# Eight heads of a gated recurrence: wide products queued in equal shares behind the score products of each level

## The chip, the cores and the metric

The kernel runs on one core of one Trainium2 chip, as one launch. The metric is the time of one execution on the device in microseconds (us); a kernel's time is the median of several runs. A profile shows one execution. Its engines are PE (TensorE, the matrix products), DVE (VectorE), ACT (ScalarE), POOL (GpSimd) and SP (SyncE, which here issues the DMAs). PEclk is the clock granted to TensorE as a share of 2.4 GHz.

## The reference

One layer of an encoder on x of 1024 positions by 1024 features, in float32. A first big product makes the inputs of two branches. Branch A is a gated linear recurrence with 8 heads of key and value size 128, run forwards and backwards; branch B is a gated MLP that mixes positions in chunks of 128. Both are merged under sigmoid gates, then come an output product, a SwiGLU and a last gated term. In short:

```
h = rms_norm(x);  z = h @ w_in                       # q, f_fwd, f_bwd, i, g, u, v, gate_a, gate_b
A = bidirectional_recurrence(q, f_fwd, f_bwd, i, g)  # 8 heads, S_t = diag(f_t) S_{t-1} + k_t v_t^T, o_t = S_t^T q_t
B = gelu(u) * mix_positions(layer_norm(gelu(v)))
mix = (sigmoid(gate_a) * (A @ w_a) + sigmoid(gate_b) * (B @ w_b)) @ w_out
x = x + rms_norm(mix);  x = x + rms_norm(swiglu(rms_norm(x)));  x = x + (p @ w_ple) * sigmoid(x @ w_ple_gate)
```

## The kernel before

Every wide product is done in three passes: each operand is split into a high and a low part (`split_into`: ScalarE copies the high part, VectorE or GpSimd subtracts for the low one), and `mm3` runs high by high, high by low and low by high for each 128 of the contraction. One such matmul is 128 x 128 by 128 x 512. The stages are: norm and first products; most columns of the first product by a seven-product scheme (`Seven`, line 283 of before for its matmuls); the head loop; the merge; the SwiGLU; the end.

The head loop runs over 8 heads. For a head, `load_head` fetches F (the forget factors of both directions), X and Y (keys) and q; `load_values` fetches v and zg. `scores` then builds the 128 x 128 score blocks of all 8 chunks without a sequential recurrence: a first group of products of q with ks = X + Y, and then seven levels (blocks of 1, 2, 4, ... 64 positions). A level is 8 small products of X with QA in two banks of PSUM called `sc`, 4 products each (TensorE shows each of these as two records). After each bank VectorE multiplies QA by the next factors of F (L612) and X likewise (L615), and merges the level's scores into SC under a mask (`copy_predicated`, L625) or ScalarE does (L622); GpSimd makes the next Y (L639), ScalarE copies it into X (L636), and VectorE halves F (L645). So QA of a level must be updated before the next level's products of the same bank, while X runs ahead by itself.

`outputs` turns the scores of a head into its output: transposes of X and Y (L662), products with v (L667), a chain of states S on VectorE (L671, L673), output products (L691), a norm over ScalarE, VectorE and GpSimd (L694, L104, L106, L698), transposes (L701), and a store to `at_d`. In the queue it falls beside the scores of the next head.

Beside each head stands wide work that has nothing to do with that head: `values` in heads 0 and 1 (counted from zero), `branch` in heads 2 and 3, `transpose_b` and a part of `branch_b` in head 4, the rest of `branch_b` in head 5, `gate_a(0)` and `gate_a(1)` in heads 6 and 7. Its products go to three PSUM banks called `mm`. The A halves that the merge needs (A0, A1) reuse the memory of h's halves, which the two calls of `gate_a` read.

What sets the order is a scheduler that goes by the program's order, the dependencies and a model of times; nothing in the kernel before says where in a head the wide work goes. Each engine then runs its queue in that order, and an instruction that waits holds up what is behind it.

Of the kernel before, what the change touches and what calls it, by code (L numbers as in the profile page):

```python
# [35 lines left out]
def kernel(ctx: ExitStack, tc: tile.TileContext, a: dict, out: bass.AP):  # L36
# [109 lines left out]
    def fm_rhs(fm):  # L146
        return lambda p, k: fm[p][k // 4][:, k % 4, :]
# [406 lines left out]
    c_t, t1 = phase("s1t", 2)  # L554
    c_tw, tmw = phase("tmw", 4)

    class Head:
        pass

    def view(t, off, dims):  # L560
        tv = t[:]
        return bass.AP(tv.tensor, tv.offset + off, [list(tv.ap[0])] + dims)
# [17 lines left out]
    def scores(h, s):  # L580
        q, X, Y, F = s.q, s.X, s.Y, s.F
        QA = hg.tile([P, 2, T], F32, name="QA", bufs=2)
        ks = hg.tile([P, T], F32, name="ks")
        SC = hg.tile([P, NT, P], F32, name="SC", bufs=2)
        nc.vector.tensor_tensor(out=QA, in0=view(q, 0, [[0, 2], [1, T]]), in1=F, op=ALU.mult)
        nc.vector.tensor_tensor(out=ks, in0=X, in1=Y, op=ALU.add)

        for g in range(2):
            sp = ps_tile("sc")
            for i in range(4):  # L590
                cs = slice((4 * g + i) * P, (4 * g + i + 1) * P)
                nc.tensor.matmul(sp[:, i * P:(i + 1) * P], lhsT=ks[:, cs], rhs=q[:, cs], start=True, stop=True)
            nc.scalar.activation(SC[:, 4 * g:4 * g + 4], sp.rearrange("p (c t) -> p c t", c=4), AF.Copy)

        for li, m in enumerate(LEVELS):
            nb = T // m
            cb = P // (2 * m)

            def level(g):
                sp = ps_tile("sc")  # L600
                for i in range(4):
                    c = 4 * g + i
                    nc.tensor.matmul(  # L603
                        sp[:, i * P:(i + 1) * P], lhsT=X[:, c * P:(c + 1) * P],
                        rhs=view(QA, c * P, [[2 * m, cb], [T + m, 2], [1, m]]), start=True, stop=True)
                return sp

            def update(g, X2):

                o, of = g * NH, g * nb // 2  # L610
                qd = [[T + m, 2], [2 * m, nb // 4], [1, m]]
                nc.vector.tensor_tensor(out=view(QA, o, qd), in0=view(QA, o, qd),  # L612
                                        in1=view(F, of + 1, [[nb - 1, 2], [2, nb // 4], [0, m]]), op=ALU.mult)
                dims = [[4 * m, nb // 8], [3 * m, 2], [1, m]]
                nc.vector.tensor_tensor(out=view(X2, o, dims), in0=view(X, o, dims),  # L615
                                        in1=view(F, nb + of + 1, [[4, nb // 8], [1 - nb, 2], [0, m]]), op=ALU.mult)

            def merge(g, sp):
                if m >= 32:
                    for p0 in range(0, P, m):  # L620
                        c0 = p0 ^ m
                        nc.scalar.activation(SC[p0:p0 + m, 4 * g:4 * g + 4, c0:c0 + m],  # L622
                                             sp.rearrange("p (c t) -> p c t", c=4)[p0:p0 + m, :, c0:c0 + m], AF.Copy)
                    return
                nc.vector.copy_predicated(  # L625
                    SC[:, 4 * g:4 * g + 4], masks[:, li, None, :].broadcast_to([P, 4, P]),
                    sp.rearrange("p (c t) -> p c t", c=4))

            X2 = hg.tile([P, T], F32, name="X", bufs=3)
            sp0 = level(0)  # L630
            update(0, X2)
            merge(0, sp0)
            sp1 = level(1)

            mid = [[4 * m, nb // 4], [1, 2 * m]]
            nc.scalar.activation(view(X2, m, mid), view(Y, m, mid), AF.Copy)  # L636
            update(1, X2)
            mid = [[4 * m, nb // 4], [m, 2], [1, m]]
            nc.gpsimd.tensor_tensor(out=view(Y, m, mid), in0=view(X, m, mid),  # L639
                                    in1=view(F, 0, [[4, nb // 4], [nb + 3, 2], [0, m]]), op=ALU.mult)  # L640
            X = X2
            merge(1, sp1)
            F2 = hg.tile([P, 2, nb // 2], F32, name=f"F{2 * m}", bufs=2 if m == 64 else 1)
            Fv = F.rearrange("p d (b h) -> p d b h", h=2)
            nc.vector.tensor_tensor(out=F2, in0=Fv[:, :, :, 0], in1=Fv[:, :, :, 1], op=ALU.mult)  # L645
            F = F2
        s.QA, s.SC, s.X, s.Y, s.F = QA, SC, X, Y, F
# [76 lines left out]

    def tm_tile(gi, t, per_tile):
        ps = ps_tile("mm")
        mm3(ps, fm_lhs(hT[t // 4], t % 4), lambda p, k: tw[gi][k // 2][:, p, k % 2, :], KD)
        per_tile(t, ps)

    def values(ts):  # L730
# [16 lines left out]
    def transpose_b(bT):  # L747
        for t in range(NT):
            if t % 2 == 0:
                raw = rawp.tile([P, 2, SGW], F32, name="ub", tag="raw")  # L750
                nc.sync.dma_start(raw, ub_d[t // 2])
            tp = ps_tile("mm")
            for i in range(4):
                nc.tensor.transpose(tp[:, i * P:(i + 1) * P], raw[:, t % 2, i * P:(i + 1) * P], ident)
            ts = slice(t % 4 * P, (t % 4 + 1) * P)
            split_into(bT[t // 4][0][:, :, ts], bT[t // 4][1][:, :, ts], tp.rearrange("p (k t) -> p k t", k=4))

    def branch_b(bT, js):
        for j0 in js:
            raw = rawp.tile([P, KD, P], F32, name="raw", tag="raw")  # L760
            for i in range(2):
                nc.sync.dma_start(raw[:, 4 * i:4 * i + 4], a["w_b"][j0 + i])
            wb = whlp.tile([P, 2, KD, P], F32R, name="whl", tag="whl")
            split_into(wb[:, 0], wb[:, 1], raw)
            for i in range(2):
                m0 = rawp.tile([P, T], F32, name="gb", tag="raw")
                nc.sync.dma_start(m0, gb_d[j0 + i])
                for n in range(2):
                    ns = slice(n * NH, (n + 1) * NH)
                    ps = ps_tile("mm")  # L770
                    mm3(ps, lambda p, k: wb[:, p, 4 * i + k, :], lambda p, k: bT[n][p][:, k, :], 4)
                    nc.vector.tensor_tensor(out=m0[:, ns], in0=ps, in1=m0[:, ns], op=ALU.mult)
                nc.sync.dma_start(m0_d[j0 + i], m0)

    def gate_a(n):
        for j in range(NGA, KD):
            w = load_split(a["w_fm"][24 + j], [KD, P], None, whlp, rawp)
            ps = ps_tile("mm")
            mm3(ps, lambda p, k: w[:, p, k, :], fm_rhs(hT[n]), KD)
            sg = t2(t1, "sk")  # L780
            nc.scalar.activation(sg, ps, AF.Sigmoid)
            nc.sync.dma_start(sig_d[j, :, n * NH:(n + 1) * NH], sg)
# [19 lines left out]
    for h in range(H):  # L802
        nxt = Head()
        scores(h, cur)
        if h + 1 < H:
            load_head(nxt, h + 1)
        if h < 2:
            if h == 1:
                tw[2] = [load_tm(2, kk, tmw, "tmw") for kk in (0, 1)]
# [5 lines left out]
        elif h == 4:  # L815
            bT = [pair(tmw, f"bT{n}", "tmw") for n in range(2)]
            transpose_b(bT)
            branch_b(bT, (0,))
        elif h == 5:
            branch_b(bT, (2, 4, 6))  # L820
        elif h == 6:

            gate_a(0)
# [335 lines left out]
```

## Time and profile before

| what | before |
|---|---|
| median of 3 runs | 2000.14 us (1999.91 to 2002.68) |
| the profiled execution | 1999.0 us, span 1997.2 us |
| TensorE busy | 1913.6 us, 96% of the span |
| VectorE busy | 1200.5 us, 60% |
| ScalarE, GpSimd busy | 737.7 us (37%), 203.7 us (10%) |
| mean granted TensorE clock | 0.982 |
| from the first score product to the merge | from 581.9 to about 1052 us of the span |

TensorE is busy for 96% of the span, so what matters is where the other 4% and the stretches of lower clock lie: of the page's 40 slices (49.9 us each) TensorE is below nine tenths only in the first, in the 14th and in the 18th to 21st, which is the second half of the head loop. A row of the timeline gives the start and the length of merged instructions; neighbours overlap a little, so the distance from start to start is what one costs in a stream.

### The profile page before, as it was taken

How to read it: one execution, taken by the hardware profiler on the slowest of the kernel's cores; microseconds unless marked ns; L12 is line 12 of the kernel's file. 1: busy time of each engine (PE TensorE's matmuls, PEld its weight loads, DVE VectorE, ACT ScalarE, POOL GpSimd, SP SyncE). 2: the span in 40 equal slices, each digit the busy share in tenths (PEclk: the TensorE clock that was granted, in tenths of full speed). 3: DMA queues.
4: the chain of work that ended last, by engine and by line, in shares of the span. 5: the costliest groups of instructions: out<-in, count | busy, mean ns of one | idle time of the engine just before them, and what ended most of it. 6: DMA issues, size and time to landing. Idle time of an engine off the chain costs nothing.

```text
span 1997.2 us, 24233 instructions
## 1 busy us (share of the span) xinstructions
PE 1913.6 (96%) x9168; PEld 1603.6 (80%) x9168; DVE 1200.5 (60%) x1870; ACT 737.7 (37%) x1383; POOL 203.7 (10%) x153
## 2 busy tenths in 40 slices
PE   7999999999999899987679999999999999999999
PEld 6878888888888888876667887788888888888887
DVE  6667756664336676788654367865545536545743
ACT  6245544443323323433332246433333324213321
POOL 2510000000022111223112201000000000001000
PEclk9999999999999999998879999999999999999999
DMA  7234434443252456443124323232222205324232
GB/s 278 70 126 154 158 128 137 138 147 113 82 207 100 159 189 231 134 141 118 43 86 167 127 89 117 91 108 70 95 85 74 85 32 194 106 75 155 89 105 80
DMA packets 94933, 243.83 MB, mean 122 GB/s; under 512 B 10080, under 2 KB 19424, under 8 KB 93792
## 3 DMA queue, kind: packets, MB, share of 16 engines
q1 hardware_dynamic: 94816, 242.28, 36.1%
q8 instruction: 72, 1.18, 0.3%
q14 instruction: 45, 0.37, 0.1%
HBM read 168.32 MB, written 73.92 MB: 121 GB/s over the span
## 4 chain that ended last, share of the span: by engine, by line
PE 87%; DVE 7%; DMA 3%; ACT 1%; issue 1%; POOL 0%; SPq 0%; DVEq 0%; ACTq 0%; POOLq 0%
PE ps_mm L283 24%; PE ps_mm L138 22%; PE ps_sc L283 12%; PE ps_sc L138 9%; PE ps_st L138 5%; PE ps_sc L603 4%; PE ps_o L283 2%; PE ps_tr L283 2%; PE ps_st L283 2%; DVE QA L612 2%; PE ps_o L691 2%; DVE X L615 1%; DMA m_d<-gb 1%; DVE SC L625 1%; PE ps_st L667 1%
## 5 line engine op out<-in xcount | busy, mean ns | idle before, releaser
L283 PE MATMUL ps_mm<-T,w 128*128 128x512 f32 x1584 | 378.5, 389 | 0.0
L283 PEld LDWEIGHTS ps_mm<-T,w 128*128 128x128 f32 x1584 | 297.3, 188 | 61.9 <-ACT u L233 0.2
L120 DVE TENSOR_TENSOR w<-sums,w 128x1024 fp32r<-128x1024 f32 x88 | 107.7, 1224 | 102.1 <-ACT w L119 102.1
L603 PE MATMUL ps_sc<-QA,X 128*128 128x128 f32 x896 | 133.3, 302 | 33.3 <-DVE QA L612 27.1
L603 PEld LDWEIGHTS ps_sc<-QA,X 128*128 128x128 f32 x896 | 124.1, 208 | 40.9 <-DVE QA L612 16.6
L119 ACT ACTIVATE w<-sums 128x1024 fp32r<-128x1024 f32 x88 | 92.8, 1056 | 119.9 <-PE ps_sc L283 83.6
L138 PE MATMUL ps_mm<-whl,act 128*128 128x512 f32 x528 | 134.1, 389 | 0.0
L283 PE MATMUL ps_sc<-T,w 128*128 128x512 f32 x528 | 131.7, 389 | 0.0
L138 PEld LDWEIGHTS ps_mm<-whl,act 128*128 128x128 f32 x528 | 99.1, 188 | 20.8
L283 PEld LDWEIGHTS ps_sc<-T,w 128*128 128x128 f32 x528 | 99.1, 188 | 20.6
L612 DVE TENSOR_TENSOR QA<-QA,F 128x512 f32<-128x512 f32 x112 | 87.5, 782 | 41.2 <-PE ps_sc L603 40.8
L119 ACT ACTIVATE whl<-raw 128x1024 fp32r<-128x1024 f32 x58 | 61.0, 1058 | 134.8 <-PE ps_sc L138 51.2
L639 POOL TENSOR_TENSOR Y<-X,F 128x512 f32<-128x512 f32 x56 | 79.2, 1414 | 293.6 <-ACT X L636 239.7
L120 DVE TENSOR_TENSOR whl<-raw,whl 128x1024 fp32r<-128x1024 f32 x50 | 69.1, 1386 | 45.6 <-ACT whl L119 45.6
L138 PE MATMUL ps_sc<-whl,act 128*128 128x512 f32 x351 | 89.9, 390 | 0.0
L138 PEld LDWEIGHTS ps_sc<-whl,act 128*128 128x128 f32 x351 | 65.7, 188 | 14.1 <-DVE act L120 0.3
L138 PE MATMUL ps_mm<-whl,hTb 128*128 128x512 f32 x312 | 75.8, 395 | 0.0
L271 DVE TENSOR_TENSOR p<-ps_mm,p 128x512 f32<-128x512 f32 x44 | 30.4, 691 | 70.6 <-PE ps_mm L283 70.6
L120 POOL TENSOR_TENSOR wpg<-raw,wpg 128x1024 fp32r<-128x1024 f32 x4 | 9.6, 2404 | 596.9 <-ACT wpg L119 596.9
L120 POOL TENSOR_TENSOR whl<-raw,whl 128x1024 fp32r<-128x1024 f32 x8 | 21.7, 2717 | 477.6 <-ACT whl L119 476.9
L138 PE MATMUL ps_mm<-whl,hTa 128*128 128x512 f32 x288 | 70.1, 397 | 0.0
L283 PE MATMUL ps_mm<-B,wA 128*128 128x512 f32 x264 | 67.2, 398 | 1.0 <-ACT wA L119 1.0
(305 smaller groups left out, 3700.4 us busy)
## 6 DMA issues: line engine op xcount, KB each, us to landing
raw<-in_w_fm_dram SPq DMA_DIRECT2D x52, 512.0 KB, 3.8
raw<-in_w_gate_dram SPq DMA_DIRECT2D x22, 512.0 KB, 3.5
raw<-in_w_up_dram SPq DMA_DIRECT2D x22, 512.0 KB, 3.8
act_d<-s SPq DMA_DIRECT2D x22, 512.0 KB, 2.9
raw<-in_w_down_dram SPq DMA_DIRECT2D x22, 512.0 KB, 4.2
raw<-act_d SPq DMA_DIRECT2D x22, 512.0 KB, 4.2
raw<-in_w_tm_dram SPq DMA_DIRECT2D x16, 512.0 KB, 5.2
F<-f_d SPq DMA_DIRECT2D x8, 1024.0 KB, 6.4
```

The lines of the kernel that those rows point to most:

```text
L119: nc.scalar.activation(hi, src, AF.Copy)
L120: (eng or nc.vector).tensor_tensor(out=lo, in0=src, in1=hi.bitcast(F32), op=ALU.subtract)
L138: nc.tensor.matmul(ps, lhsT=lhs(lp, k), rhs=rhs(rp, k), start=(i == 0), stop=(i == n - 1))
L271: nc.vector.tensor_tensor(out=c22, in0=X, in1=c22, op=ALU.add)
L283: nc.tensor.matmul(ps, lhsT=lhs(lp, k), rhs=rhs(rp, k), start=(first and i == 0), stop=(i == n - 1), skip_group_check=True)
L603: nc.tensor.matmul(sp[:, i * P:(i + 1) * P], lhsT=X[:, c * P:(c + 1) * P], rhs=view(QA, c * P, [[2 * m, cb], [T + m, 2], [1, m]]), start=T ...
L612: nc.vector.tensor_tensor(out=view(QA, o, qd), in0=view(QA, o, qd), in1=view(F, of + 1, [[nb - 1, 2], [2, nb // 4], [0, m]]), op=ALU.mult)
L615: nc.vector.tensor_tensor(out=view(X2, o, dims), in0=view(X, o, dims), in1=view(F, nb + of + 1, [[4, nb // 8], [1 - nb, 2], [0, m]]), op=A ...
L625: nc.vector.copy_predicated(SC[:, 4 * g:4 * g + 4], masks[:, li, None, :].broadcast_to([P, 4, P]), sp.rearrange("p (c t) -> p c t", c=4))
L639: nc.gpsimd.tensor_tensor(out=view(Y, m, mid), in0=view(X, m, mid), in1=view(F, 0, [[4, nb // 4], [nb + 3, 2], [0, m]]), op=ALU.mult)
L667: nc.tensor.matmul(up[:, i * P:(i + 1) * P], lhsT=kt[:, i], rhs=v[:, c], start=True, stop=True)
L691: nc.tensor.matmul(op[:, i * P:(i + 1) * P], lhsT=l, rhs=r, start=(j == 0), stop=(j == len(terms) - 1))
```

## The change

A class `Pace` gives every wide product of a head a mark: the last score product of the first group, or the last one of a level's second bank. `tc.issue_after(mark)` adds an edge that puts the product behind that mark in TensorE's queue. There are eight marks a head, and product i of n gets mark i * 8 // n, so each mark has the same share: 12 of 96 products, in head 4 13 of 104 (32 transposes and 72 products), in head 5 15 of 120. `mm3` of the wide work becomes `pace.mm3`, and `branch_b` runs over single columns instead of pairs, three of them in head 4 and five in head 5 (before: two and six). The products themselves, the loads and the stores are as before.

```diff
+    class Pace:
+        def __init__(self, marks, n):
+            self.marks, self.n, self.i = marks, n, 0
+
+        def mm3(self, ps, lhs, rhs, nk):
+            n = nk * len(PASSES)
+            i = 0
+            for k in range(nk):
+                for lp, rp in PASSES:
+                    with tc.issue_after(self.next()):
+                        nc.tensor.matmul(ps, lhsT=lhs(lp, k), rhs=rhs(rp, k), start=(i == 0), stop=(i == n - 1))
+                    i += 1
+
+        def next(self):
+            mark = self.marks[min(self.i * len(self.marks) // self.n, len(self.marks) - 1)]
+            self.i += 1
+            return mark
...
-                nc.tensor.matmul(sp[:, i * P:(i + 1) * P], lhsT=ks[:, cs], rhs=q[:, cs], start=True, stop=True)
+                mark = nc.tensor.matmul(sp[:, i * P:(i + 1) * P], lhsT=ks[:, cs], rhs=q[:, cs], start=True, stop=True)
             nc.scalar.activation(SC[:, 4 * g:4 * g + 4], sp.rearrange("p (c t) -> p c t", c=4), AF.Copy)
+        s.marks = [mark.ins]
...
-                    nc.tensor.matmul(
+                    mark = nc.tensor.matmul(
                         sp[:, i * P:(i + 1) * P], lhsT=X[:, c * P:(c + 1) * P],
                         rhs=view(QA, c * P, [[2 * m, cb], [T + m, 2], [1, m]]), start=True, stop=True)
+                if g == 1:
+                    s.marks.append(mark.ins)
...
-        mm3(ps, fm_lhs(hT[t // 4], t % 4), lambda p, k: tw[gi][k // 2][:, p, k % 2, :], KD)
+        pace.mm3(ps, fm_lhs(hT[t // 4], t % 4), lambda p, k: tw[gi][k // 2][:, p, k % 2, :], KD)
...
-                nc.tensor.transpose(tp[:, i * P:(i + 1) * P], raw[:, t % 2, i * P:(i + 1) * P], ident)
+                with tc.issue_after(pace.next()):
+                    nc.tensor.transpose(tp[:, i * P:(i + 1) * P], raw[:, t % 2, i * P:(i + 1) * P], ident)
...
-            mm3(ps, lambda p, k: w[:, p, k, :], fm_rhs(hT[n]), KD)
+            pace.mm3(ps, lambda p, k: w[:, p, k, :], fm_rhs(hT[n]), KD)
...
+        pace = Pace(cur.marks, {4: 104, 5: 120}.get(h, 96))
...
-            branch_b(bT, (0,))
+            branch_b(bT, range(3))
         elif h == 5:
-            branch_b(bT, (2, 4, 6))
+            branch_b(bT, range(3, KD))
```

Two places of TensorE's queue show the move. The first is where the stage of the seven-product scheme ends (L283) and head 0's scores begin. Before, wide products of `values` (L138, weights `whl` against h) stand even ahead of the last twelve products of L283, and the scores come a hundred wide products later:

```order
L283 MATMUL ps_sc<-hTb_164,w_4205 128x512
L283 MATMUL ps_sc<-hTb_162,w_4205 128x512
L138 MATMUL ps_mm<-whl,hTa_157 128x512 x2
L138 MATMUL ps_mm<-whl,hTa_159 128x512
L138 MATMUL ps_mm<-whl,hTa_157 128x512 x2
L138 MATMUL ps_mm<-whl,hTa_159 128x512
L138 MATMUL ps_mm<-whl,hTa_157 128x512 x3
```

Now the first score group (L613, which was L592) follows the stage's last product, and the wide ones (L570, which were L138) come behind it and behind the first level (L625, which was L603):

```order
L283 MATMUL ps_mm<-T_917,w_4208 128x512
L283 MATMUL ps_mm<-T_916,w_4208 128x512
L613 MATMUL ps_sc<-q,ks 128x128 x8
L570 MATMUL ps_mm<-whl,hTa_157 128x512 x2
L570 MATMUL ps_mm<-whl,hTa_159 128x512
L570 MATMUL ps_mm<-whl,hTa_157 128x512 x2
L570 MATMUL ps_mm<-whl,hTa_159 128x512
L570 MATMUL ps_mm<-whl,hTa_157 128x512 x2
L570 MATMUL ps_mm<-whl,hTa_159 128x512
L570 MATMUL ps_mm<-whl,hTa_157 128x512 x2
L570 MATMUL ps_mm<-whl,hTa_159 128x512
L625 MATMUL ps_sc<-QA,X_4332 128x128 x8
```

What moved: nothing wide is left between the two stages, and 12 products stand behind the first group.

The second place is head 6. Before, no wide product is left there; the first group, the levels and pieces of the previous head's outputs follow each other:

```order
L592 MATMUL ps_sc<-q,ks 128x128 x8
L603 MATMUL ps_sc<-QA,X_6701 128x128 x8
L701 MATMUL ps_tr<-ident,on 128x128 x4
L691 MATMUL ps_o<-v,SC 128x128
L603 MATMUL ps_sc<-QA,X 128x128 x4
L662 MATMUL ps_tr<-ident,X 128x128
```

Now `gate_a(0)` stands in that head, with 12 products behind each group, of which the last ones behind its first level are these, followed by transposes of the outputs (L686, which was L662) and the next level:

```order
L625 MATMUL ps_sc<-QA,X_6738 128x128 x4
L570 MATMUL ps_mm<-hTa_158,whl 128x512
L570 MATMUL ps_mm<-hTa_160,whl 128x512
L570 MATMUL ps_mm<-hTa_158,whl 128x512 x2
L570 MATMUL ps_mm<-hTa_160,whl 128x512
L570 MATMUL ps_mm<-hTa_158,whl 128x512 x2
L570 MATMUL ps_mm<-hTa_160,whl 128x512
L570 MATMUL ps_mm<-hTa_158,whl 128x512 x2
L570 MATMUL ps_mm<-hTa_160,whl 128x512
L570 MATMUL ps_mm<-hTa_158,whl 128x512
L686 MATMUL ps_tr<-ident,X 128x128
L686 MATMUL ps_tr<-ident,Y 128x128
```

What moved: a share of 12 wide products now stands between the level and what follows it.

## Rows read from the trace of the kernel before

**Rows 1.** Stretches, one head each: length, busy us (instructions), clock, DMA

```profile
581.90:647.70 65.80, 65.80 (x361) 57.30 (x360) 37.95 (x56) 21.74 (x39) 15.30 (x10) 1.00 0.37 121
647.70:711.60 63.90, 58.87 (x367) 53.18 (x365) 45.38 (x81) 22.80 (x62) 11.95 (x10) 0.95 0.45 152
711.60:774.50 62.90, 61.61 (x378) 54.45 (x377) 45.12 (x79) 17.79 (x51) 10.78 (x9) 1.00 0.61 206
774.50:840.50 66.00, 63.03 (x385) 55.84 (x385) 46.77 (x79) 29.64 (x67) 13.11 (x10) 1.00 0.54 183
840.50:885.80 45.30, 37.54 (x256) 34.24 (x255) 36.59 (x60) 16.77 (x51) 10.67 (x9) 0.96 0.33 114
885.80:925.80 40.00, 32.23 (x227) 30.24 (x225) 35.56 (x64) 14.98 (x46) 12.53 (x9) 0.91 0.30 104
925.80:962.70 36.90, 25.74 (x171) 23.81 (x171) 34.33 (x59) 12.55 (x29) 10.06 (x8) 0.86 0.35 120
962.70:1044.70 82.00, 57.06 (x329) 51.74 (x328) 42.95 (x76) 26.36 (x83) 13.62 (x11) 0.79 0.19 61
```

**Rows 2.** TensorE's longest wait, 555 to 1070: total us, times, longest

```profile
PE ps_sc L603 <- DVE QA L612: 27.1, 15, 4.1
```

**Rows 3.** TensorE's timeline, head zero: start, length, instruction, count

```profile
617.27 5.70 PE L138 MATMUL ps_mm<-whl,hTa 128*128 128x512 f32 x24
622.81 1.95 PE L603 MATMUL ps_sc<-QA,X 128*128 128x128 f32 x16
624.51 5.70 PE L138 MATMUL ps_mm<-whl,hTa 128*128 128x512 f32 x24
```

**Rows 4.** TensorE's timeline in head five, the wait in brackets

```profile
908.75 3.76 PE L603 MATMUL ps_sc<-QA,X 128*128 128x128 f32 x16 [3.57 <-DVE QA L612]
```

**Rows 5.** TensorE's timeline ahead of the first score product

```profile
556.21 4.92 PE L138 MATMUL ps_mm<-whl,hTa 128*128 128x512 f32 x21
560.97 2.88 PE L283 MATMUL ps_mm<-T,w 128*128 128x512 f32 x12
563.69 17.46 PE L138 MATMUL ps_mm<-whl,hTa 128*128 128x512 f32 x75
```

**Rows 6.** VectorE's timeline: the loop's start, the split at its end

```profile
556.01 0.69 DVE L271 TENSOR_TENSOR p<-ps_mm,p 128x512 f32<-128x512 f32 x1 [4.30 <-PE ps_mm L283]
...
571.20 1.95 DVE L645 TENSOR_TENSOR F<-F 128x1024 f32<-128x1024 f32 x2 [4.51 <-DMA F<-f_d]
...
576.92 1.22 DVE L586 TENSOR_TENSOR ks<-X,Y 128x1024 f32<-128x1024 f32 x1
...
1044.72 1.29 DVE L120 TENSOR_TENSOR A<-rawA,A 128x512 fp32r<-128x512 f32 x2 [2.75 <-ACT A L119]
```

**Rows 7.** SyncE's timeline: F of head zero, rawA at the end

```profile
564.93 0.38 SPq L566 DMA_DIRECT2D F<-f_d  x1
...
1039.04 0.32 SPq L790 DMA_DIRECT2D rawA<-at_d  x1
```

**Rows 8.** TensorE's timeline at the loop's end

```profile
1034.52 1.25 PE L701 MATMUL ps_tr<-ident,on 128*128 128x128 f32 x4 [2.93 <-ACT on L698]
...
1052.13 5.04 PE L138 MATMUL ps_sc<-A,whl 128*128 128x512 f32 x21
```

**Rows 9.** The page's costliest groups: GpSimd's Y products

```profile
L639 POOL TENSOR_TENSOR Y<-X,F 128x512 f32<-128x512 f32 x56 | 79.2, 1414 | 293.6 <-ACT X L636 239.7
```

**Rows 10.** VectorE's groups, 563.7 to 1070: busy us, mean ns, idle before

```profile
L120 DVE TENSOR_TENSOR whl<-raw,whl 128x1024 fp32r<-128x1024 f32 x18 | 24.5, 1363 | 21.5 <-ACT whl L119 21.5
...
L772 DVE TENSOR_TENSOR gb<-ps_mm,gb 128x512 f32<-128x512 f32 x16 | 10.9, 684 | 2.4 <-PE ps_mm L138 2.1 <-issue 0.2
```

**Rows 11.** The chain that ended last, 720 to 740: start, length

```profile
727.95 6.13 DMA m_d<-gb
...
734.48 3.19 DMA raw<-in_w_b_dram
```

**Rows 12.** The line of the X products: ns min/median/max

```profile
L615 DVE TENSOR_TENSOR X<-X,F x112: 398/419/1744, 573.1 to 1012.9; 128x256 f32<-128x256 f32 x112
```

More of the change, by code (lines that the diff above doesn't have):

```diff
@@ L753, in transpose_b @@
             for i in range(4):
-                nc.tensor.transpose(tp[:, i * P:(i + 1) * P], raw[:, t % 2, i * P:(i + 1) * P], ident)
+                with tc.issue_after(pace.next()):
+                    nc.tensor.transpose(tp[:, i * P:(i + 1) * P], raw[:, t % 2, i * P:(i + 1) * P], ident)
             ts = slice(t % 4 * P, (t % 4 + 1) * P)
             split_into(bT[t // 4][0][:, :, ts], bT[t // 4][1][:, :, ts], tp.rearrange("p (k t) -> p k t", k=4))
+    wb = {}
     def branch_b(bT, js):
[L759 to L773, printed above, removed]
+        for j in js:
+            if j % 2 == 0:
+                raw = rawp.tile([P, KD, P], F32, name="raw", tag="raw")
+                for i in range(2):
+                    nc.sync.dma_start(raw[:, 4 * i:4 * i + 4], a["w_b"][j + i])
+                wb[0] = whlp.tile([P, 2, KD, P], F32R, name="whl", tag="whl")
+                split_into(wb[0][:, 0], wb[0][:, 1], raw)
+            m0 = rawp.tile([P, T], F32, name="gb", tag="raw")
+            nc.sync.dma_start(m0, gb_d[j])
+            for n in range(2):
+                ns = slice(n * NH, (n + 1) * NH)
+                ps = ps_tile("mm")
+                pace.mm3(ps, lambda p, k: wb[0][:, p, 4 * (j % 2) + k, :], lambda p, k: bT[n][p][:, k, :], 4)
+                nc.vector.tensor_tensor(out=m0[:, ns], in0=ps, in1=m0[:, ns], op=ALU.mult)
+            nc.sync.dma_start(m0_d[j], m0)
     def gate_a(n):
```

## The prediction

> **What bounds the kernel now.** I read the table of stretches by head first. TensorE is busy all through the first head (65.80 of 65.8 us), nearly so through the next three, and then thins out: 37.54 of 45.3, 32.23 of 40.0, 25.74 of 36.9 and 57.06 of 82.0 us in heads four to seven (counted from zero), with the granted clock down to 0.96, 0.91, 0.86 and 0.79 [rows 1]. Differences of the columns give 61 us of idle TensorE over the eight heads. The list of waits says who is late most: the vector engine's update of QA (L612), 27.1 us in 15 waits [rows 2]. The timeline shows why early heads don't suffer: 24 wide products (5.5 us to the next start) stand between two levels there [rows 3], while a head without them waits 3.57 us for QA and then runs 16 score records in 3.76 us [rows 4] where 1.95 is usual [rows 3]. So the wide work is spent on the heads where it stands too thick, and the last three and a half heads run at the vector engine's pace: 40.0 and 36.9 us for heads five and six, with that engine busy 35.56 and 34.33 us [rows 1].
>
> **The change, part by part.** No product, copy or transfer is added or dropped. 768 wide products and 32 transposes stand elsewhere: 12 products (in head four 13 instructions, in head five 15) behind the last score product of each of the eight groups of a head. That takes work from where it hid something and puts it where TensorE idles.
>
> *The start loses its cover.* Before, some hundred wide products ran ahead of the first score product; 21 of them even ahead of the last twelve products of the stage before, the rest from 563.69 on [rows 5]. Now nothing may run there. The last twelve move up by 4.76 us (556.21 to 560.97), less about 0.5 us, since the vector engine reads their bank until 556.70 [rows 5, 6]: 4.2 us. What the first score product needs did not move against them: F is asked for at 564.93 [rows 7], right after the stage ends at 563.69; the vector engine starts on it at 571.20 and ends ks at 576.92 + 1.22 = 578.14 [rows 6]. That is 14.45 us after the stage's end, now bare. The first score product starts at 563.7 - 4.2 + 14.45 = 573.9 instead of 581.9. Beside the rows: the Trainium skill (TensorE: Matmul & The Clock Gate, "What you observe") says that TensorE's default state is throttled and sustained activity releases it. Here the trace agrees: after 3.57 us of idling, the records at 908.75 ran at half pace [rows 4].
>
> *TensorE's work from there on.* Level: 1.70 us from 622.81 to 624.51 for 16 records, 0.106 each. Wide product: 5.54 us / 24 = 0.231 [rows 3]. I run the sum to the transposes of head six's second output half (before at 1034.52 [rows 8]): 64 groups x 1.70 = 108.8; 768 x 0.231 = 177.4; 32 transposes 3.5; 36 products of the merge that the new order puts there 8.3; outputs of seven heads, 94 records x 0.11 each, 72.4; four early transposes 0.4. Together 370.8 us, so 944.7 without any wait, against 1034.5.
>
> *The end.* From these transposes to the merge's first run of 21 products it took 1052.13 - 1034.52 = 17.6 us [rows 8]. A transfer chain goes through it: the half output is stored, rawA is read back from 1039.04 [rows 7], and the vector engine splits it at 1044.72, with the last S steps queued behind the split [rows 6]. That chain is the same now: its 10.2 us from 1034.52 to the split can't shrink, so I keep 17.6, between 14 and 20. The last splits of A1 and of w_a now fall beside it, since gate_a(1) ends later; they have 46 wide products to hide under. 944.7 + 17.6 = 962.3 against 1052.1: 89.8 us saved, if nothing waits.
>
> *What will wait.* (a) A slow clock after the bare start: the stretch at 908.75 lost 3.76 - 1.95 = 1.8 us after 3.57 us of idling [rows 3, 4]. Head seven gives the other end: 0.21 of its 57.06 busy us, 12.0, were lost over 24.9 idle ones [rows 1], 0.48 for each, 7.0 for 14.45. I take 3, nearer to the single gap. (b) In the first head the scalar engine frees the second score bank behind a copy that waits for GpSimd: 2 us, between 0 and two Y of 1.41 us on GpSimd [rows 9]. (c) The vector engine. A head without wide work cost 40.0 and 36.9 us [rows 1], say 38.5, with that engine full. Add what the wide work brings it, with 0.684 us for each result of 128x512, as gb has, and 1.363 for each split of 128x1024, as whl has [rows 10]: heads one to three at most 2.7 us (four products with sg); head four 8 splits of bT 5.5, two of weights 2.7, six gb 4.1: 12.3; head five ten gb and two weights, 9.5; head six four weights and three of A, 9.5; head seven six and three, 12.3. Floors: up to 41.2, then 50.8, 48.0, 48.0, 50.8. TensorE needs 13.6 + 22.2 + 10.3 = 46.1 in heads one, two, three, six and seven, 44.0 in head four, 51.6 in head five. Where the floor is higher the head takes the floor: 6.8 + 1.9 + 4.7 = 13.4 us. (d) In branch_b each weight pair waits until an earlier gb has been stored and its buffer is read anew: 6.13 us and 3.19 us on the chain [rows 11], then 2.4 us of splits. That is 11.7 us beside 24 products, which are a fifth of head five's 120 and so now last a fifth of its 51.6 us, 10.3: 1 to 2 us late for each of three pairs, 5 us, between 0 and 12. (e) Where both engines stand within a few us, meetings are missed. Heads one to three idled 5.0, 1.3 and 3.0 us with much thicker cover [rows 1]; the scalar engine's output, one of the causes, now has 12 to 24 products over it, so I take 1.5 us a head, 10.5 in all, between 0 and 3.1 a head (22). Sum of the waits: 3 + 2 + 13.4 + 5 + 10.5 = 33.9 us.
>
> One thing speaks against the change: GpSimd's seven products Y a head, 1.41 us each [rows 9]. The vector engine's X products take 0.398 us at least, 0.419 in the middle, and 1.744 at most [rows 12]: the longest lost 1.33 us, nearly a whole Y. The floor of 38.5 contains what was lost so. If every Y stopped the vector engine wholly, it would be 7 x 1.41 = 9.9 us a head, so the floor can rise by 0 to 9.9; the forecast takes 0, since in heads five and six that engine was as full as it will be now. The Trainium skill (SBUF — State Buffer, "SBUF: two separate sides") says that the two engines share one port pair as an exclusive lock, held for a whole instruction; the long X products agree [rows 12]. By that rule a busier vector engine meets more of them; it stands behind the second rival.
>
> **The sum.** 89.8 - 33.9 = 55.9 us saved. The profiled execution took 1999.0 us (span 1997.2), the median of the runs is 2000.14, 1.1 more: 1999.0 - 55.9 + 1.1 = 1944.
>
> **Rivals.** *All is covered.* Only the start's price stays: 89.8 - 3 = 87 saved, 1913 us. For it: TensorE never idled in the first head [rows 1]. Against: there it had twice the products between levels. 0.14.
>
> *The vector engine sets the pace of every head.* With 5 us more a head, half of the 9.9 above, heads one to three rise to the 46 us that TensorE needs, and all others pay: four heads x 5 = 20, with head five's partly free (3.6 of it): 16 to 20, and the meetings at their upper bound, 11.5 more: 28 to 31 us over the forecast, 1973. For it: 35.56 of 40.0 us busy in a head that never had cover [rows 1]. Against: its own queue holds work of the next head to fill in. 0.24.
>
> *The shares add to the chain instead of covering it (the slower side).* Place: between a level's last score product and the next level's first. If the QA update started only after the 12 products, because products and evictions in the scalar and vector queues hold it back, a head would cost 38.5 + 22.2 = 60.7 us: seven heads are 14.6 each over 46.1, 102 us in place of the 28.9 of (c), (d) and (e); with 5 us for the start 107 over the bare sum, 17 lost: 2017 us. It decides from 89.8 / 56 = 1.6 us of wait before each level. Against: the update waits for score records alone, which stand ahead of the share [rows 4]. 0.05.
>
> *It doesn't do what it says.* The mark is a lower bound, and products could be issued far later. The new order shows 12 after nearly every group, so I give it 0.02, near no change.
>
> **Chances.** Forecast 0.55, at 1928 to 1961 for itself: (c) and (e) at their ends. All covered 0.14, vector pace 0.24, added chains 0.05, nothing 0.02. The range that holds 8 in 10 reaches most of the way to both neighbours: 1917 to 1978. Within 0.2% (4 us, about what a measurement of this kernel can tell from no change) lies nearly only the last case. Faster 0.93, same 0.02, slower 0.05.
>
> **What would show it.** In the new trace: TensorE idle for some 14 us ahead of the first score product, at about 560; heads of 46 to 52 us with TensorE over 85% busy and the granted clock at 0.97 or more; waits for QA under 1 us each, most of them in heads four, six and seven; the merge's run of 21 products near 995. Wrong would be: heads over 55 us, waits for QA before each level, a start gap under 5 us, or a stall after the last head of more than 5 us on w_a or A1.

## The result and the profile after

The changed kernel takes 1976.66 us in the median of its runs (1975.76 to 1977.67) against 2000.03 of the kernel before beside it: a ratio of 0.9887, with a 95% interval of 0.9865 to 0.991. It is faster by some 23 us, inside the predicted range and less than half of the 56 us of the forecast. The profiled execution took 1975.76 us, its span 1974.0, at a mean granted clock of 0.985.

The loop by stretches, one for each head from its first score product to the next head's, the last one to the transposes of head six's second output half; the columns are those of [rows 1], to which they answer:

```profile
573.30:623.30 50.00, 43.38 (x242) 38.22 (x243) 36.44 (x55) 14.72 (x29) 16.43 (x10) 0.92 0.26 91
623.30:671.50 48.20, 46.58 (x305) 41.97 (x305) 38.66 (x62) 18.93 (x54) 14.90 (x10) 1.00 0.36 110
671.50:721.70 50.20, 47.91 (x314) 42.94 (x313) 37.92 (x70) 18.08 (x50) 11.62 (x9) 1.00 0.34 119
721.70:768.90 47.20, 45.40 (x293) 40.82 (x293) 35.66 (x68) 15.34 (x34) 11.25 (x8) 1.00 0.34 120
768.90:820.00 51.10, 43.67 (x289) 38.48 (x288) 42.03 (x72) 20.46 (x57) 9.53 (x8) 0.93 0.51 177
820.00:888.30 68.30, 62.94 (x384) 55.63 (x384) 51.66 (x88) 20.18 (x55) 15.87 (x11) 0.95 0.54 188
888.30:945.70 57.40, 49.29 (x301) 43.60 (x300) 41.15 (x67) 24.54 (x59) 11.69 (x9) 0.91 0.52 179
945.70:1012.64 66.94, 63.72 (x406) 56.85 (x405) 43.21 (x71) 30.45 (x85) 11.41 (x10) 0.97 0.31 103
sum 439.34, PE 402.88 PEld 358.52 DVE 326.73 ACT 162.70 POOL 102.72; mean PE 50.36 PEld 44.82 DVE 40.84 ACT 20.34 POOL 12.84
```

Heads one to four have become alike (47 to 51 us), as the change says, and TensorE is busy for 402.88 of 439.34 us. But heads five to seven are still long, and the clock is at 0.91 to 0.97 from head four on. TensorE's longest waits from 550 to 1050 us (total, times, longest), the first QA row answering to [rows 2]:

```profile
PE ps_sc L613 <- DVE ks L607: 14.5, 1, 14.5
PE ps_sc L625 <- DVE QA L636: 13.6, 11, 2.9
PE ps_sc L625 <- issue: 7.7, 2, 4.2
PE ps_sc L625 <- ACT on L718: 4.9, 2, 2.4
```

The waits for QA's updates have halved, from 27.1 us to 13.6. New is the bare start (14.5). There are also four waits ahead of a head's first level, one in each of heads four to seven, 7.7 + 4.9 = 12.6 us; before there was one such, 2.43 us at 983.55 in head seven. The vector engine's timeline shows what the building of QA (L606) stands behind in heads four, six and seven:

```profile
776.15 2.29 DVE L606 TENSOR_TENSOR QA<-q,F 128x2048 f32<-128x2048 f32 x1 [0.51 <-PE ps_o L715]
...
895.90 1.23 DVE L120 TENSOR_TENSOR whl<-raw,whl 128x1024 fp32r<-128x1024 f32 x1 [6.10 <-ACT whl L119]
897.04 0.74 DVE L727 SCALAR_TENSOR_TENSOR on<-ps_tr,vec,zg 128x512 f32<-128x512 f32 x1
897.70 2.28 DVE L606 TENSOR_TENSOR QA<-q,F 128x2048 f32<-128x2048 f32 x1
...
955.51 2.29 DVE L606 TENSOR_TENSOR QA<-q,F 128x2048 f32<-128x2048 f32 x1 [1.70 <-PE ps_o L715]
```

In head six a weight split waits 6.10 us for the scalar engine, and the building of QA (2.28 us) stands behind it in the vector engine's queue; TensorE's level starts at 900.08, when QA is there. In head five a split (from 835.09) stands just ahead of it too. In heads four and seven the building itself waits for output products (L715): QA has two buffers, and these products read the one that it takes. After the wait in head six the granted clock is 0.50, the lower of its two levels, as this stretch shows (columns as above):

```profile
900.00:908.00 8.00, 6.84 (x26) 6.13 (x27) 3.35 (x6) 2.43 (x5) 1.01 (x1) 0.50 0.87 310
```

Start and end of the loop on TensorE, answering to [rows 5] and [rows 8]:

```profile
555.80 3.01 PE L283 MATMUL ps_mm<-T,w 128*128 128x512 f32 x12 [0.39 <-DVE p L271]
573.30 2.08 PE L613 MATMUL ps_sc<-q,ks 128*128 128x128 f32 x8 [14.49 <-DVE ks L607]
...
1012.64 0.60 PE L725 MATMUL ps_tr<-ident,on 128*128 128x128 f32 x4
...
1027.53 5.06 PE L138 MATMUL ps_sc<-A,whl 128*128 128x512 f32 x21
```

| part | forecast | measured |
|---|---|---|
| first score product | 573.9 | 573.30 |
| head zero | 41.2 | 50.0 |
| heads one to three | 142.8 | 145.6 |
| head four | 52.3 | 51.1 |
| head five | 58.1 | 68.3 |
| head six | 49.5 | 57.4 |
| head seven, to the transposes | 60.8 | 66.9 |
| from there to the merge | 17.6 | 14.9 |
| merge's first run | 996.2 | 1027.5 |

The forecast's column is the prediction's own terms, put to the heads: 36.2 + 3 + 2 for head zero, 46.1 + 1.5 for one, two and three, then the floors or TensorE's need with 1.5 for meetings, 5 more in head five and the merge's 8.3 in head seven (and 0.2 of rounding there). The start, heads one to four and the end are right within 3 us each; heads zero, five, six and seven are 33 us too long.

### The profile page after: what moved, and what is told of

It is laid out like the page before. It is cut to its first block, busy times and chain, and to the rows that moved or that the text cites. A ratio compares the mean times of both kernels' runs of the same rounds, so it can differ in the third digit from the quotient of the medians.

```text
span 1974.0 us, 24221 instructions
## 1 busy us (share of the span) xinstructions
PE 1896.6 (96%) x9168; PEld 1587.3 (80%) x9168; DVE 1203.0 (61%) x1870; ACT 738.2 (37%) x1383; POOL 205.3 (10%) x153
## 4 chain that ended last, share of the span: by engine, by line
PE 87%; DVE 6%; DMA 3%; ACT 1%; issue 1%; POOL 1%; SPq 0%; DVEq 0%; POOLq 0%; ACTq 0%
PE ps_mm L283 24%; PE ps_mm L138 15%; PE ps_sc L283 12%; PE ps_sc L138 9%; PE ps_mm L570 7%; PE ps_sc L625 5%; PE ps_st L138 5%; PE ps_o L283 2%; PE ps_tr L283 2%; PE ps_st L283 2%; PE ps_o L715 1%; DVE QA L636 1%; PE ps_st L691 1%; PE ps_sc L613 1%; DVE X L639 1%
## 5 line engine op out<-in xcount | busy, mean ns | idle before, releaser
L283 PE MATMUL ps_mm<-T,w 128*128 128x512 f32 x1584 | 378.6, 389 | 0.4 <-DVE p L271 0.4
L283 PEld LDWEIGHTS ps_mm<-T,w 128*128 128x128 f32 x1584 | 297.1, 188 | 62.7 <-DVE p L271 0.8
L625 PE MATMUL ps_sc<-QA,X 128*128 128x128 f32 x896 | 126.0, 292 | 26.9 <-DVE QA L636 13.6
L625 PEld LDWEIGHTS ps_sc<-QA,X 128*128 128x128 f32 x896 | 116.9, 200 | 33.6 <-issue 17.1
L138 PE MATMUL ps_mm<-whl,act 128*128 128x512 f32 x528 | 134.1, 389 | 0.0
L283 PE MATMUL ps_sc<-T,w 128*128 128x512 f32 x528 | 131.7, 389 | 0.0
L138 PEld LDWEIGHTS ps_mm<-whl,act 128*128 128x128 f32 x528 | 99.1, 188 | 20.7
L283 PEld LDWEIGHTS ps_sc<-T,w 128*128 128x128 f32 x528 | 99.1, 188 | 20.6
L138 PE MATMUL ps_sc<-whl,act 128*128 128x512 f32 x351 | 89.7, 390 | 0.0
L138 PEld LDWEIGHTS ps_sc<-whl,act 128*128 128x128 f32 x351 | 65.8, 188 | 13.9 <-ACT acc L1046 0.3
L660 ACT ACTIVATE X<-Y 128x512 f32<-128x512 f32 x56 | 36.2, 646 | 100.2 <-PE ps_sc L625 79.2
L283 PE MATMUL ps_mm<-B,wA 128*128 128x512 f32 x264 | 67.2, 398 | 1.3 <-ACT wA L119 1.3
L283 PE MATMUL ps_sc<-hTb,w 128*128 128x512 f32 x264 | 66.3, 389 | 0.0
```

The lines of the kernel that those rows point to most:

```text
L138: nc.tensor.matmul(ps, lhsT=lhs(lp, k), rhs=rhs(rp, k), start=(i == 0), stop=(i == n - 1))
L283: nc.tensor.matmul(ps, lhsT=lhs(lp, k), rhs=rhs(rp, k), start=(first and i == 0), stop=(i == n - 1), skip_group_check=True)
L625: mark = nc.tensor.matmul(sp[:, i * P:(i + 1) * P], lhsT=X[:, c * P:(c + 1) * P], rhs=view(QA, c * P, [[2 * m, cb], [T + m, 2], [1, m]]), ...
```

## The experiments

Ratios are to the kernel before on the same chip, with 95% intervals; the changed kernel's own is 0.9887 (0.9865 to 0.991), and 0.001 is 2 us. On these chips the kernel before took 2000 to 2006 us in the median, and a ratio carries that spread. The other kernels' traces show no such spread between chips: from the merge's first run to the end they all take 945 to 948 us. So a number of us won or lost is here the difference of medians to the changed kernel's 1976.66 us, unless the text says otherwise, and the table at the end of this section has all three measures. No run shows the changed kernel on a second chip, so a us or two between kernels of different chips says nothing. Theory A, at first: the building of QA, the start and the places of the waits cost the time. Theory B: the vector engine's amount of work does.

**Vector engine relieved, QA in halves, start covered.** In e1 the merge under the mask is left out, so these scores are not merged:

```diff
-                nc.vector.copy_predicated(SC[...], masks[...], sp...)
+                return
```

> The paced kernel with the 80 masked merges of scores into SC (copy_predicated, levels 1 to 16) left out: 57.8 us of VectorE's work by the trace of before, some 7 us a head. Theory A (an order and buffer chain at each change of head makes the waits: QA of the next head can't be built before the outputs of the head before last are done): the waits ahead of a head's first level in heads 4 to 7 (2.4, 3.5, 4.3 and 2.4 us) stay over 1.5 us each, and the time falls by less than 10 us from 1976. Theory B (VectorE's throughput sets the pace of heads 4, 6 and 7, as term (c) of the prediction has it): heads 4, 6 and 7 become 4 to 7 us shorter each and the time falls by 15 to 25 us.

In e2 QA is two tiles, so that the first half is free and built earlier:

```diff
-        QA = hg.tile([P, 2, T], F32, name="QA", bufs=2)
+        QA = [hg.tile([P, 2, NH], F32, name=f"QA{g}", bufs=2) for g in range(2)]
```

> QA as two tiles of half the positions, each with two buffers, in the same memory, so that a half can be built for the head after next as soon as the first output half has been computed. VectorE's elements are the same, eight instructions more. Theory A: the waits ahead of the first level of heads 4 to 7 (12.6 us in sum) shrink under 1 us each, the slow clock behind them goes too, and the time falls by 10 to 20 us from 1976. Theory B (VectorE's throughput): no change beyond 4 us.

In e3 the first 60 products of head zero carry no mark, and e4 is e2 and e3 together:

```diff
-        pace = Pace(cur.marks, {4: 104, 5: 120}.get(h, 96))
+        pace = Pace(cur.marks, {4: 104, 5: 120}.get(h, 96), 60 if h == 0 else 0)
```

> The first 60 products of head 0 carry no mark, so they may run ahead of the first score product; the other 36 are spread over its eight marks, 4 or 5 each. Theory A: the idle 14.5 us at the start shrink under 1.5 us, head 0 falls from 50.0 to 39 to 43 us, since VectorE needs that long for it, and the net gain is 7 to 13 us from 1976. Rival (head 0 needs its twelve products as cover): head 0 waits for QA in every level, gives the gain back and the time stays within 4 us.

> Both edits: the first 60 products free, and QA in two halves. Theory A: the two gains lie in different heads and add: 17 to 33 us below 1976, so 1943 to 1959. Rival (VectorE's throughput takes over as the bound): less than 10 us.

Measured: e1 0.9779 (0.9757 to 0.9801), e2 0.9894 (0.9874 to 0.9915), e3 0.9893 (0.9859 to 0.9927), e4 0.9877 (0.9857 to 0.9896). Only e1 moved, by 21 us, which was B's number; A fell. But B's places were wrong as well: head four, which it had 4 to 7 us shorter, took 53.0 us instead of 51.1, and head five, which it did not name, 60.1 instead of 68.3. In e2 the waits ahead of the first level did go, but another stood in their place, for the norm of the outputs; and e3's first head had the shorter gap and yet a lower clock than the changed kernel's 0.92. First the longest of e2's waits from 550 to 1050 us, then e3's first score products on TensorE's timeline, then e3's head zero as a stretch:

```profile
PE ps_tr L727 <- ACT on L724: 19.4, 7, 4.5
```

```profile
578.30 3.78 PE L617 MATMUL ps_sc<-q,ks 128*128 128x128 f32 x16 [5.09 <-DVE ks L611]
```

```profile
578.30:621.08 42.78, 32.46 (x183) 29.01 (x184) 35.42 (x50) 13.46 (x28) 16.15 (x10) 0.82 0.31 108
```

Head zero shrank from 50.0 to 42.8 us, but it began 5.0 us later, so that head one began only 2.2 us earlier. Head seven began 8.6 us earlier, took 12.6 us longer up to the merge's first run, and e3 as a whole won nothing: what was won was given back late. That asked for the loop to be tested by halves.

**The two halves.** e5 and e6 leave the merges out of heads 0 to 3 or of heads 4 to 7; e7 and e8 issue every fourth wide product twice (`twice`) in the one half or the other.

```diff
+                if h >= 4:          # e5; e6: h < 4
                     nc.vector.copy_predicated(SC[...], masks[...], sp...)
```

```diff
+                        for _ in range(2 if self.twice and i % 4 == 1 else 1):
                             nc.tensor.matmul(ps, lhsT=lhs(lp, k), rhs=rhs(rp, k), ...)
```

> The masked merges (copy_predicated, 0.69 us each, 10 a head) are left out of heads 0 to 3 only, so the scores of those heads are not merged; some 27 us less of the vector engine there. Theory L (the loop has two halves: heads 0 to 3 run at TensorE's pace, heads 4 to 7 at the vector engine's, and what is won early is mostly given back late): the merge starts 0 to 6 us earlier than in the changed kernel, 1971 to 1977 us. Theory U (both engines bind in every head alike, so half of the 21 us that leaving out all merges won): 1964 to 1968 us.

> The masked merges are left out of heads 4 to 7 only (those scores are not merged), some 27 us less of the vector engine there. Theory L (late heads at the vector engine's pace): 15 to 21 us won, 1956 to 1962 us, with heads 4 to 7 shorter by 4 to 6 us each. Theory U (both engines bind alike in every head): 8 to 13 us, 1964 to 1969 us.

> Every fourth wide product of heads 0 to 3 is issued twice (it is then counted twice in its sum), 96 products more, 96 x 0.229 = 22 us more of TensorE. Theory L (early heads at TensorE's pace, but lateness there is partly made up later): heads 0 to 3 longer by 4 to 5.5 us each, and 12 to 22 us in all, 1989 to 1999 us. Theory U (two engines bind alike): about half, 9 to 13 us, 1986 to 1990 us.

> Every fourth wide product of heads 4 to 7 is issued twice (and counted twice), 104 products and transposes or so more, 22 us more of TensorE there. Theory L (late heads at the vector engine's pace, TensorE with slack): 0 to 8 us slower, 1977 to 1985 us, idle TensorE in these heads down from 24 us. Theory U: 9 to 13 us slower. If TensorE's own work sets these heads too, as the sum of the forecast has it for head five: 15 to 24 us slower, 1992 to 2001 us.

Measured: e5 0.9779 (0.9752 to 0.9806), e6 0.9812 (0.9791 to 0.9834), e7 0.9927 (0.9901 to 0.9952), e8 0.9854 (0.9831 to 0.9878). Theory L missed on e5: leaving out the merges of the early heads alone won 16 us, three quarters of e1's 21. Theory U missed it too, in size and in place, for the time went where nothing had been taken out. e6 won 9 us, which is U's number and half of L's. e7 paid 15 of its 22 us, as L had it: heads zero to three grew by 20, heads four to six shrank by 11 and the last, up to the merge, grew by 10. e8 paid nothing in the median and 3.7 us in the trace, near L too. So neither theory fits all four. Heads four to six of e5 as stretches, and after them their sum in the changed kernel:

```profile
769.11:822.72 53.61, 48.95 (x328) 43.78 (x326) 47.00 (x80) 22.13 (x60) 12.27 (x9) 0.97 0.53 192
822.72:880.16 57.44, 54.23 (x343) 48.27 (x342) 45.52 (x80) 18.31 (x51) 11.94 (x10) 1.00 0.56 193
880.16:929.39 49.23, 46.59 (x300) 41.15 (x299) 40.53 (x65) 22.73 (x49) 10.80 (x8) 1.00 0.61 218
sum 160.28, PE 149.76 PEld 133.21 DVE 133.05 ACT 63.18 POOL 35.01; mean PE 49.92 PEld 44.40 DVE 44.35 ACT 21.06 POOL 11.67
```

```profile
sum 176.73, PE 155.82 PEld 137.64 DVE 134.80 ACT 65.19 POOL 37.05; mean PE 51.94 PEld 45.88 DVE 44.93 ACT 21.73 POOL 12.35
```

Its heads zero to three took 196.6 us, the changed kernel's 195.6: the relief won nothing there. Heads four to six do the same work in both, and the vector engine is busy for 133.05 against 134.80 us, yet they take 16.4 us less. e8 points the same way: 96 products (22 us) more in heads four to seven cost it next to nothing. These heads and the merge's start take 261.3 us there against 258.6; TensorE idles 13.5 instead of 27 us, and its clock costs 6 instead of 12 (busy time by one less the clock, head by head). So neither engine's amount of work alone set these heads. What differs is the order of the queues, which the scheduler writes anew for each kernel. On TensorE's timeline of the changed kernel 20 of head four's products stand behind head five's first score products, and head three's output products come only after them (a head's output products, L715, stand about the start of the head after next):

```profile
819.38 0.71 PE L570 MATMUL ps_mm<-bT,whl 128*128 128x512 f32 x2
819.98 1.16 PE L613 MATMUL ps_sc<-q,ks 128*128 128x128 f32 x8
820.90 4.79 PE L570 MATMUL ps_mm<-bT,whl 128*128 128x512 f32 x20
825.53 0.83 PE L613 MATMUL ps_sc<-q,ks 128*128 128x128 f32 x6
826.19 0.39 PE L715 MATMUL ps_o<-S,QA 128*128 128x128 f32 x2
...
838.62 2.05 PE L625 MATMUL ps_sc<-QA,X 128*128 128x128 f32 x8 [3.49 <-issue]
```

**GpSimd's products, and the order at the end.** e9 takes the lines of Y out, so its Y is not updated. e10 is e4 with the merge's first 36 products held behind head six's outputs (`wait` lists the last output product of either half):

```diff
-            nc.gpsimd.tensor_tensor(out=view(Y, m, mid), in0=view(X, m, mid), in1=view(F, ...), op=ALU.mult)
```

```diff
+                first = Pace([wait[j]], 3 * KD).mm3 if j < 2 and n == 0 else mm3
-                mm3(ps, lambda p, k: wa[j][:, p, k, :], fm_rhs(A[n]), KD)
+                first(ps, lambda p, k: wa[j][:, p, k, :], fm_rhs(A[n]), KD)
```

> GpSimd's products Y (1.41 us each, 7 a head) are left out, so the half of Y that they make stays unset by them and the state takes the old values there; all else stands. If GpSimd's products hold the vector engine up, as the second rival has it (5 us a head in the four heads that it paces), the vector engine's X products lose their long cases and 10 to 25 us are won, 1952 to 1967 us. If the vector engine is late by its own work alone: 0 to 5 us, 1972 to 1977 us.

> The kernel with QA in halves and 60 free products in head 0 (e4), and besides the 36 products of the merge that need no late head held behind head six's output products, 18 behind each half, where in e4 they stood ahead of both. Theory T (e4 reached head seven 18 us ahead and gave it back because the order put 36 products, 8.3 us, ahead of head six's outputs and left their norm chains bare, 2.9 us each before the transposes): the outputs start 8 us earlier and the two bare waits shrink to under 1.5 us, so 6 to 10 us faster than e4, 1965 to 1970 us. Theory V (the end hangs on the vector engine's work in the last heads, whatever the order of the products): within 3 us of e4, 1972 to 1979 us.

Measured: e9 0.9825 (0.9784 to 0.9867), e10 0.9824 (0.9787 to 0.986). GpSimd does hold the vector engine up. Two of that engine's groups from 573 to 1012 us, of the changed kernel and of e9:

```profile
L636 DVE TENSOR_TENSOR QA<-QA,F 128x512 f32<-128x512 f32 x112 | 91.0, 815 | 48.0 <-PE ps_sc L625 47.1
L639 DVE TENSOR_TENSOR X<-X,F 128x256 f32<-128x256 f32 x110 | 59.2, 574 | 2.2 <-PE ps_tr L686 1.7 <-ACT X L660 0.5
```

```profile
L636 DVE TENSOR_TENSOR QA<-QA,F 128x512 f32<-128x512 f32 x112 | 78.3, 700 | 49.5 <-PE ps_sc L625 48.7
L639 DVE TENSOR_TENSOR X<-X,F 128x256 f32<-128x256 f32 x109 | 44.5, 444 | 1.7 <-PE ps_tr L683 1.7
```

In heads zero to three it is busy for 148.7 us in the changed kernel and 130.0 in e9, 4.7 a head, for the same instructions. These heads took 190.3 instead of 195.6 us, and e9 as a whole won 7 us (12 by the ratio, whose interval touches the changed kernel's), less than its first theory's 10 and more than the other's 5; its order differs as well, and what that did was not separated. e10 is 5.4 us faster than e4 (10.6 by the ratio, and the intervals touch), just under theory T's 6. On TensorE's timeline e4 had the merge's products first and then both norms bare, the second at 1008.02 with the same 2.93 us; e10, in the second fence, has the products between:

```profile
990.40 4.38 PE L138 MATMUL ps_mm<-A,whl 128*128 128x512 f32 x18
...
999.94 1.25 PE L731 MATMUL ps_tr<-ident,on 128*128 128x128 f32 x4 [2.93 <-ACT on L728]
```

```profile
994.60 4.38 PE L571 MATMUL ps_mm<-A,whl 128*128 128x512 f32 x18
998.81 0.60 PE L732 MATMUL ps_tr<-ident,on 128*128 128x128 f32 x4
```

**The order alone.** e11 changes one mark of the changed kernel and leaves nothing out. `out` lists the last output product of each half, which by the kernel's loop is the eleventh of the first half. e12 adds the free start of e3 and the end of e10.

```diff
+        if h in range(3, 4):
+            cur.marks[7] = prv.out[0]
```

> One mark differs from the changed kernel: the last 12 wide products of head three may be queued only behind head two's first ten output products, and not behind the last level alone. Nothing is left out. The order of the queues that follows has heads four to six as in e5: head three's outputs start inside head four, and no 20 products of head four slip into head five. Theory O (e5 and e1 won in heads four to seven by the order that the planner wrote when the merges were gone, not by the vector engine's time): 13 to 21 us won, 1956 to 1964 us. Theory B (it was the vector engine's time): within 4 us of the changed kernel, 1973 to 1981 us.

> e11 with the first 60 products of head zero free, as in e3, and 36 products of the merge held behind head six's output products, 18 behind each half, as in e10. If the order in the late heads was what gave the start's gain back in e3, and with theory O as in e11: e11's gain and 5 to 10 us more from the start (start gap 5 in place of 14.5 us, first score product 5 us later), 1948 to 1957 us. If an early gain is always given back: e11's time within 4 us.

Measured: e11 0.9833 (0.9816 to 0.985), e12 0.9821 (0.9804 to 0.9838), medians 1968.6 and 1966.8 us. e11's interval lies wholly below the changed kernel's, and so do all its six runs (1967.0 to 1975.3 us): one mark for 12 products is worth 8 us (11 by the ratio), between theory B's 4 and O's 13. The 20 products no longer slip, and head three's output products start inside head four, as e11's timeline of TensorE shows:

```profile
821.04 0.38 PE L715 MATMUL ps_o<-S,QA 128*128 128x128 f32 x2
...
824.98 3.21 PE L570 MATMUL ps_mm<-bT,whl 128*128 128x512 f32 x13
828.02 1.72 PE L613 MATMUL ps_sc<-q,ks 128*128 128x128 f32 x14
```

```profile
sum 166.45, PE 152.27 PEld 134.58 DVE 132.64 ACT 64.43 POOL 36.77; mean PE 50.76 PEld 44.86 DVE 44.21 ACT 21.48 POOL 12.26
```

The second fence is the sum of e11's heads four to six as stretches, 10.3 us less than in the changed kernel, where e5's were 16.4 less. Idle time fell from 20.9 to 14.2 us there, and what the clock cost from 10.6 to 2.9; the busy time less that cost grew by 4. So about half of what e5 won can be won by the order alone. The rest, 6 us of these heads and 2 us elsewhere, may be the vector engine's time or what still differs in the order; this was not separated. Of e12's expected 5 to 10 us beyond e11 only 1.8 came, within the intervals: its head zero is 7 us shorter, its head seven with the end 4 us longer. e10 and e12 beat both kernels, by 7 and 10 us over the changed one (13 by the ratios), and can't be told apart.

All runs; the last column is where the merge's first run of 21 products starts in the trace, less the changed kernel's 1027.53. It has one execution of each, and it goes with the median within 5 us:

| run | ratio to before | median, us | less 1976.66 | merge's first run |
|---|---|---|---|---|
| e1 no merges | 0.9779 | 1955.75 | -20.9 | -23.9 |
| e2 QA in halves | 0.9894 | 1979.17 | +2.5 | +3.5 |
| e3 60 products free | 0.9893 | 1978.50 | +1.8 | +3.9 |
| e4 both | 0.9877 | 1975.55 | -1.1 | -2.0 |
| e5 no merges, heads 0 to 3 | 0.9779 | 1960.55 | -16.1 | -14.4 |
| e6 no merges, heads 4 to 7 | 0.9812 | 1967.85 | -8.8 | -10.2 |
| e7 more products, heads 0 to 3 | 0.9927 | 1991.39 | +14.7 | +15.4 |
| e8 more products, heads 4 to 7 | 0.9854 | 1975.47 | -1.2 | +3.7 |
| e9 no Y | 0.9825 | 1969.28 | -7.4 | -7.4 |
| e10 e4 and the end | 0.9824 | 1970.14 | -6.5 | -7.5 |
| e11 one mark | 0.9833 | 1968.60 | -8.1 | -6.3 |
| e12 e11, start and end | 0.9821 | 1966.80 | -9.9 | -8.9 |

## Why the prediction was right in sign and too large

**The start** was right: 14.45 us bare forecast, 14.49 measured, and the first score product at 573.30 for 573.9.

**TensorE's work was mis-sized**, 370.8 us forecast and 386.9 measured. The second number is busy time less what the clock cost: 402.9 - 16.0, the latter busy time by one less the clock, stretch by stretch. The instructions are those that the forecast counted. It took the price of a level from one stretch, 1.70 us for 16 records [rows 3]. The first level of a head is dearer, and so are the shares:

```profile
628.65 1.49 PE L625 MATMUL ps_sc<-QA,X 128*128 128x128 f32 x8
629.84 0.77 PE L570 MATMUL ps_mm<-whl,hTb 128*128 128x512 f32 x2
...
630.93 1.59 PE L625 MATMUL ps_sc<-QA,X 128*128 128x128 f32 x8
632.22 3.04 PE L570 MATMUL ps_mm<-whl,hTb 128*128 128x512 f32 x12
635.10 0.83 PE L691 MATMUL ps_st<-v,kt 128*128 128x128 f32 x6
```

Eight records of the first level take 1.19 and 1.29 us to the next start, where half of 1.70 is 0.85: 0.78 us a head, 6 in all. A share of 12 takes 2.88 us here (and 2.82 from 949.59 in head seven), where half of 5.54 is 2.77: 64 shares make 3 to 7 us. The rest was not traced. Little of this is lost by the change: counted the same way, the kernel before was at work for 391.9 us from 563.69 to 1034.52, with 21 of these products done already. So some 16 of the 89.8 us that "nothing waits" would save were never idle there.

**The clock (a) failed as a step**: 3 us forecast, 16.0 measured. The forecast let it fall only after the start, and gave the other waits no price for it. Its own 0.48 us for each idle one [rows 1], put on the 30.9 us of waits (b) to (e) that it forecast, would have been 15 us more, about what was missing. The clock fell in head zero and in all of heads four to seven, where TensorE idles for 3 to 8 us a head. The start gap alone doesn't set it in head zero either: with 5.09 us of it left, e3 had a clock of 0.82 there, beside 10.3 us of idling among thinner shares. Nor is the clock a matter of a head's idle sum alone: e4's head four idled for 6.7 of 49.2 us and ran at 1.00.

**The waits (b) to (e)** were 30.9 us in sum and 36.4 measured (439.3 - 402.9), with other places. Heads one to three came as said, 145.6 us for 142.8. In head zero (b) had 2 us for a score bank; measured were 6.6 us, in three waits for QA's updates. Head four came out at 51.1 us for 52.3, but that was luck: 20 of its products ran in head five, and in e11, where they did not, it took 57.9. What failed is that each late head was priced by itself, with 1.5 us for meetings. The order carried work and lateness from one to the next: half of head three's output products and the 20 products ran in head five, which for all its 68.3 us idled no more than priced (5.4 us for 6.5), and the building of QA in heads four to seven stood behind a split or behind output products. Head six idled for 8.1 us instead of 3.4. e11 gets 10.3 us of heads four to six back by 12 products' place, with all work kept.

**The end** took 14.9 us for 17.6. In sum: 16.1 of work, 13.0 of clock and 5.5 of waits too little, 2.7 for the end and 0.6 for the start too much: 31.3, the difference of 1027.5 and 996.2.

**The rivals.** *All is covered* fell with the waits. *The vector engine sets the pace of every head* (1973) came nearest in time. The loss to GpSimd's products is real, 4.7 us a head of the vector engine's busy time in e9 for the rival's 5. But leaving them out won 7 us in all, not the 16 to 20 that it priced for the late heads, and in heads four to six e9 took only 3.9 us less than the changed kernel, while the order alone gave e11 10.3 there. Heads one to three kept TensorE's pace, which this rival had as well. The rule that stood behind it, the Trainium skill's shared port as an exclusive lock (SBUF — State Buffer, "SBUF: two separate sides"), agrees with e9, where X's products last 444 ns in the mean, and 574 with Y beside them. *The shares add to the chain* fell: QA's waits halved. Of the signs of being wrong one came, heads over 55 us (five, six, and seven even without the merge's products).

## What to carry to other kernels

When a scheduler writes the queues, an edit that takes work from one engine also rewrites the order, so a leave-out experiment alone can't tell throughput from order: look whether the time went where the work was taken, and then reproduce the order with all work kept. A ratio to a kernel that itself varies by some us is too coarse for gains of that size: set it beside the medians and the traces. Sum the engine's work at prices from several kinds of stretch, since waiting that is really work can't be saved. And price idling twice where the clock drops with it, once as idle time and once as the slower stretch that follows.

## What the runs showed that was not expected

- 22 us more of TensorE's work in heads four to seven cost at most 4 us (median 1975.47 against 1976.66, the merge 3.7 us later in the trace): idle time fell by 14 us and the clock's loss by 6.
- The place of 12 products in head three shortened heads five and six, 50 us later and more, by 17 us (68.3 + 57.4 to 57.9 + 50.6), while head four grew by 7.
- Matmuls of the first level, whose QA operand is read in blocks of one position, take some 0.165 us a record from start to start instead of 0.11 (8 records last 1.49 to 1.59 us and not 1.06), in the kernel before as well (1.49). That the blocks are the reason was not tested.
